# Sampled tokens: keys turned by transposes of 128 columns, weights times values on four column groups, memory values as the stationary operand

## The chip, the cores and the metric

The kernel runs on one core of a Trainium2 chip. The metric is the device time of one execution in microseconds (us). TensorE multiplies: it holds a stationary operand (at most 128 rows by 128 columns) that a weight load puts there, and streams a moving operand past it; the result lands in PSUM, on the partitions that belong to the stationary operand's columns. VectorE (DVE), ScalarE (ACT) and GpSimd (POOL) do the rest of the arithmetic, SyncE (SP) issues most DMAs, and each engine works through its own instructions in order.

## The reference

The program is one inference step of a two-layer decoder: 1024 prompt tokens, and 8 sampled tokens (one for each of 8 sequences) that stand behind a cache of 8192 tokens. Each layer projects the normalized input, runs four groups of heads side by side, and projects their gated results back. Cut to what matters for a sampled token:

```python
def nsa_mix(q, kc, vc, ks, vs, kw, vw, ...):     # 4 heads of 64, one key head
    kcc, vcc = compress_rows(kc, ...), compress_rows(vc, ...)   # 32 tokens -> 1 row
    p_c = masked_softmax(q . kcc); o_c = p_c @ vcc
    idx = top_k(score(p_c), 16)                   # 16 blocks of 64 tokens
    o_s = softmax(q . ks[idx]) @ vs[idx]          # selected tokens
    o_w = softmax(q . kw) @ vw                    # last 512 tokens
    return gates . (o_c, o_s, o_w)
# memory head, per sequence: 4 heads of 64, 256 memory rows
o_m = softmax(q . k_mem) @ v_mem
```

Every sequence has caches of its own, so for the 8 sampled tokens the keys and values differ while there are only 4 query rows (heads) for each.

## The kernel before

Each layer has a projection stage, prompt attention, a stage that compresses the paged cache (tiles `ct`, `ch`, `R`: gathered rows are transposed and multiplied with the compression weights), and an output stage in which the prompt rows go through the output weights in three products of high and low halves (tile `oa`, lines 120 to 122). The sampled tokens' work is laid between these: the window branch (`sample_window`, tile `W`) and the memory head (`mem_sample`) in the compression stage, the compressed and selected branches (`sample_select`, tiles `Vc`, `G`, `H`) in the output stage. A scheduler with priorities and a simulated timeline of its own sets each engine's order when the program is built, so an edit moves other work too.

`s_tokens` takes two samples at a time. Keys lie as tokens by 64; scores need them as 64 by tokens, the even sample's on partitions 0 to 63 and the odd one's on 64 to 127 of one PSUM tile `mt`. The even ones are transposes (`tr`, L246), the odd ones products of the key tile with an identity (L948). One fp32 product leaves two records in the trace, one transpose leaves one. All 32 query rows (8 samples by 4 heads) then meet each pair of samples with zeros where sample and query do not match.

`s_pv` transposes the weights (`PT`) and multiplies them, 32 columns wide, with the values of all 8 samples side by side, 512 columns, chunk after chunk into partitions 0 to 31 of tile `ma` (L908). A row's own sample is one of the eight blocks of 64; VectorE masks with `g4` (`oh`, L913) and adds up the blocks (`pvx`, L916). The new token's share comes from a small product (L911), which VectorE adds (L918). Per layer the function runs on 2 chunks of `Vc`, 4 chunks of `W`, and 6 of `G` with 2 of `H`.

`mem_sample` multiplies weights into the values on GpSimd (L1204), adds the two chunks of 128 rows (L1205), and sums over rows on TensorE with a column of ones as moving operand (L1207). Its result `msoy` is stored to a buffer `od` in HBM, which the output stage reads back (`oo` for prompt rows, `so` for the sampled ones, with `oz` and `sz` from the gates); `wof` are the output weights, `ox` the residual.

Of the kernel before, what the change touches and what calls it, by code (L numbers as in the profile page):

```python
# [9 lines left out]
F32 = mybir.dt.float32  # L10
# [6 lines left out]
OP = mybir.AluOpType  # L17
AX = mybir.AxisListType
# [6 lines left out]
NB = 8  # L25
# [15 lines left out]
def _const_array():  # L41
    cols = {}
    parts = []
    at = 0

    def put(name, a):
        nonlocal at
        a = np.asarray(a, np.float32)
        full = np.zeros((128, a.shape[1]), np.float32)
        full[:a.shape[0]] = a  # L50
        cols[name] = (at, a.shape[1])
        parts.append(full)
        at += a.shape[1]

    i = np.arange(128)
    put("ident", np.eye(128))
    put("causT", (i[:, None] <= i[None, :]))
    t = 128 * np.arange(NT)[None, :] + i[:, None]
    n = np.arange(32)
    put("vcmp", (t >= 31))  # L60
    inv = (10000.0 ** (-np.arange(32, dtype=np.float64) / 32)).astype(np.float32)
    pos = np.concatenate([t, np.full((128, 1), 8192)], 1).astype(np.float32)
    ang = (pos[:, :, None] * inv[None, None, :]).astype(np.float64)
    b32 = np.arange(32) // 4
    put("g4", b32[:, None] == np.arange(8)[None, :])
    put("moff", np.where(b32[:, None] == np.arange(8)[None, :], 0.0, NEG))
    put("iota64", np.tile(np.arange(64), (8, 1)))
    put("tok2", (2 * (i % 64))[:, None])
    put("i32", (i % 32)[:, None])
    put("bd16", np.repeat(np.eye(8), 16, 1))  # L70
    w = np.array([[2, 8], [4, 16]])[i // 64]
    put("invw", 1.0 / w)
    cnt = np.minimum(w[:, :, None], np.arange(16)[None, None, :] + 1)
    put("invc", (1.0 / cnt).reshape(128, -1))
    put("bones", (i[:, None] // 64) == (i[None, :] // 64))
    at1 = at
    put("mcmp", np.where(32 * n[None, None, :] + 31 <= t[:, :, None], 0.0, NEG).reshape(128, -1))
# [35 lines left out]
class Net:  # L113
# [772 lines left out]
    def s_pv(self, P, ks, V, sc, sp, new=None):  # L886


        nc = self.nc
        nch, full = len(ks), ks.count(128)  # L890
        PT = sp.tile([128, nch, 32], F32, name=f"PT{nch}")
        ps = self.psT()
        at = 0
        for c, k in enumerate(ks):
            self.tr(ps[:k, c * 32:c * 32 + 32], P[:, at:at + k])
            at += k
        if new is not None:
            self.tr(ps[:NB, nch * 32:nch * 32 + 32], P[:, at:])
            pnT = sp.tile([NB, 32], F32, name="pnT")
            nc.vector.tensor_copy(pnT, ps[:NB, nch * 32:nch * 32 + 32])  # L900
        nc.vector.tensor_copy(PT[:, :full].rearrange("p c q -> p (c q)"), ps[:, :full * 32])
        if full < nch:
            k = ks[full]
            nc.vector.tensor_copy(PT[:k, full:].rearrange("p c q -> p (c q)"), ps[:k, full * 32:nch * 32])

        O = self.psA()
        for c, k in enumerate(ks):
            nc.tensor.matmul(O[:32], PT[:k, c], V(c), start=c == 0, stop=c == nch - 1)  # L908
        pn = ps[:32, 448:512]
        if new is not None:  # L910
            nc.tensor.matmul(pn, pnT, new, start=True, stop=True)  # L911
        t = sp.tile([32, NB, 64], F32, name="oh", bufs=1)
        nc.vector.tensor_tensor(t, O[:32].rearrange("p (b d) -> p b d", d=64),  # L913
                                self.c("g4")[:32].unsqueeze(2).to_broadcast([32, NB, 64]), op=OP.mult)
        x = sp.tile([32, 64], F32, name="pvx", bufs=1)
        nc.vector.tensor_reduce(x, t.rearrange("p b d -> p d b"), axis=AX.X, op=OP.add)  # L916
        if new is not None:
            nc.vector.tensor_tensor(x, pn, x, op=OP.add)  # L918
        nc.vector.scalar_tensor_tensor(self.s_R, x, sc, self.s_R, op0=OP.mult, op1=OP.add)

    def s_tokens(self, K, V, ks, br, grp, sp):

        nc = self.nc
# [11 lines left out]
        for p in range(nb // 2):  # L935
            for S, (c0, m) in zip(Sg, cs):
                ln = sum(m)
                kh, kl = [sp.tile([128, 512], F32R, name=f"kt{x}", tag=f"kt{x}", bufs=2) for x in "hl"]
                ps = self.psT()
                for e in range(2):  # L940
                    at = 0
                    for c, k in enumerate(m):
                        to = ps[e * 64:e * 64 + 64, at:at + k]
                        x = K(2 * p + e, c0 + c)
                        if e == 0:
                            self.tr(to, x)
                        else:
                            nc.tensor.matmul(to, x, self.ident[:k, :k], start=True, stop=True)  # L948
                        at += k
                nc.scalar.copy(kh[:, :ln], ps[:, :ln])  # L950
                nc.vector.tensor_tensor(kl[:, :ln], ps[:, :ln], kh[:, :ln].bitcast(F32), op=OP.subtract)
# [13 lines left out]
    def sample_window(self, l, sp):  # L965
        W = sp.tile([128, NB, 4, 128], F32, name="W")
        for b in range(NB):
            self.nc.sync.dma_start(W[:, b], self.a["cache_nsa_win"][l, b].rearrange("(c p) k o d -> p c (k o d)", p=128))
        self.s_tokens(lambda b, c: W[:, b, c, 0:64], lambda c: W[:, :, c, 64:], [128] * 4, 2, (0, NB), sp)

    def sample_select(self, l, grp, sp):

# [43 lines left out]
        nc.vector.tensor_copy(ptf, pti)  # L1016
        for c in range(2):
            cs = slice(8 * c, 8 * c + 8)
            oh = sp.tile([32, NB, 64], F32, name="oh", bufs=1)[:nb]
# [26 lines left out]
        for b in range(nb):  # L1046
# [9 lines left out]
        self.s_tokens(lambda b, c: G[:, b, c // 2, c % 2, 128:192] if c < 6 else H[:, b, c % 2, 0:64],  # L1056
                      lambda c: G[:, :, c // 2, c % 2, 192:] if c < 6 else H[:, :, c % 2, 64:], [128] * 6 + [96] * 2, 1, grp, sp)

    def sample_out(self, sp):
# [111 lines left out]
    def mem_sample(self, l, wk):  # L1171
# [26 lines left out]
        PT = wk.tile([128, 2, 32], F32, name="msPT")  # L1198
        nc.vector.tensor_copy(PT.rearrange("p c q -> p (c q)"), pt[:, :64])

        O = self.psA()
        for b in range(NB):
            v = V[:, b].rearrange("p c (h d) -> p c h d", d=64)
            nc.gpsimd.tensor_tensor(v, v, PT[:, :, b * 4:b * 4 + 4].unsqueeze(3).to_broadcast([128, 2, 4, 64]), op=OP.mult)  # L1204
            nc.gpsimd.tensor_tensor(V[:, b, 0], V[:, b, 0], V[:, b, 1], op=OP.add)  # L1205
            for hp in range(2):
                mm(O[:, hp * NB + b:hp * NB + b + 1], V[:, b, 0, hp * 128:hp * 128 + 128], self.ones[:, 0:1],  # L1207
                   start=True, stop=True)
        oy = wk.tile([128, 2, NB], F32, name="msoy")
        nc.vector.tensor_copy(oy.rearrange("p c b -> p (c b)"), O[:, :2 * NB])  # L1210
        for c in range(2):
            self.oput(6 + c, T, NB, oy[:, c])

# [587 lines left out]
```

## Time and profile before

| what | value |
|---|---|
| median of 3 runs | 2343.73 us (2340.57 to 2345.09) |
| the profiled execution | 2343.6 us, its span 2341.8 us |
| TensorE busy | 87% of the span (weight loads 78%) |
| VectorE, ScalarE, GpSimd busy | 65%, 38%, 32% |
| mean granted TensorE clock | 0.93 |
| chain that ended last | TensorE 58%, VectorE 16%, DMA 11% |

The span runs from the first to the last instruction of the profiled execution; 1.8 us of its time lie around it. A busy share is an average over stages. The chain is followed back from the last instruction: at each step it goes to what released that instruction, or to the one before it on its engine.

### The profile page before, as it was taken

The page shows a single profiled execution, that of the slowest core. Times are in us where ns is not written, and L with a number is a line of the kernel's source. Part 1 is how long each engine was busy: PE and PEld are TensorE (multiplying, and loading weights), DVE is VectorE, ACT ScalarE, POOL GpSimd, SP SyncE. Part 2 cuts the span into 40 slices and gives each one's busy share as a digit, 9 for nine tenths or more (in the row PEclk, how much of TensorE's full clock was granted, in tenths as well). Part 3 has the DMA queues.
Part 4 walks back from the last instruction along what each step waited for, and adds up shares of the span by engine and source line. Part 5 has one row for each costly group of instructions (what it writes and reads, how often), then busy time and mean ns, then how long its engine had stood idle before and what let it go on. Part 6 is the DMA issues. An engine that isn't in the chain of part 4 may idle for free.

```text
span 2341.8 us, 41952 instructions
## 1 busy us (share of the span) xinstructions
PE 2048.5 (87%) x14396; PEld 1824.7 (78%) x14396; DVE 1511.6 (65%) x3927; ACT 888.2 (38%) x2221; POOL 746.7 (32%) x841
## 2 busy tenths in 40 slices
PE   4999998894798999896979999898949899998878
PEld 4997888784788888785669979887838888878645
DVE  7874377885777666553298724788867776656523
ACT  4223366553433323230152234675545333333101
POOL 2002123313655543223020012243146555532340
PEclk8999999997899899898989999999969998998889
DMA  7237321106655446776253363221086544467661
GB/s 249 92 109 184 94 78 52 58 26 169 176 146 149 119 125 184 201 235 200 87 171 105 112 155 98 66 61 47 28 208 170 140 135 136 138 190 221 174 206 51
DMA packets 324093, 312.97 MB, mean 134 GB/s; under 512 B 60619, under 2 KB 285783, under 8 KB 323608
## 3 DMA queue, kind: packets, MB, share of 16 engines
q1 hardware_dynamic: 261544, 213.25, 31.1%
q0 software_dynamic: 24320, 79.71, 11.7%
q10 hardware_dynamic: 38016, 17.32, 2.8%
q8 instruction: 115, 1.88, 0.3%
q14 instruction: 98, 0.80, 0.1%
HBM read 255.00 MB, written 59.57 MB: 134 GB/s over the span
## 4 chain that ended last, share of the span: by engine, by line
PE 58%; DVE 16%; DMA 11%; issue 8%; ACT 3%; POOL 2%; SPq 2%; ACTq 0%; DVEq 0%; another core or an unknown queue 0%; POOLq 0%
PE ch L120 3%; PE ch L122 3%; PE mt L246 3%; PE ct L246 3%; PE ch L121 3%; PE aa L121 3%; PE aa L122 3%; PE aa L120 3%; PE mt L1429 2%; PE oa L122 2%; PE oa L120 2%; PE oa L121 2%; DVE P L804 2%; PE fa L120 2%; PE fa L122 2%
## 5 line engine op out<-in xcount | busy, mean ns | idle before, releaser
L524 POOL DMA_INDIRECT R<-in_cache_nsa_dram,idxc x256 | 253.1, 989 | 295.8 <-PE ct L246 192.5
L120 PE MATMUL ch<-w1h,Xh 128*128 128x256 f32 x1024 | 314.3, 307 | 17.6 <-ACT Xh L564 8.7
L122 PE MATMUL ch<-w1h,Xl 128*128 128x256 f32 x1024 | 311.4, 304 | 6.1 <-DVE Xl L565 3.2
L121 PE MATMUL ch<-w1l,Xh 128*128 128x256 f32 x1024 | 308.7, 301 | 0.4 <-issue 0.4
L120 PEld LDWEIGHTS ch<-w1h,Xh 128*128 128x128 f32 x1024 | 209.1, 204 | 23.5 <-ACT Xh L564 10.2
L122 PEld LDWEIGHTS ch<-w1h,Xl 128*128 128x128 f32 x1024 | 208.4, 204 | 13.8 <-DVE Xl L565 5.7
L148 POOL TENSOR_TENSOR wl<-wf,wh 128x1024 fp32r<-128x1024 f32 (+2 forms) x42 | 94.9, 2271 | 377.1 <-ACT wh L139 295.6
L564 ACT CAST Xh<-ct 128x512 fp32r<-128x512 f32 x256 | 146.0, 585 | 180.0 <-PE ct L246 109.9
L121 PEld LDWEIGHTS ch<-w1l,Xh 128*128 128x128 f32 x1024 | 209.0, 204 | 2.0 <-issue 0.4
L565 DVE TENSOR_TENSOR Xl<-ct,Xh 128x512 fp32r<-128x512 f32 x256 | 172.4, 683 | 42.8 <-ACT Xh L564 26.1
L246 PE MATMUL ct<-cst,R 128*128 128x128 f32 x1024 | 163.9, 292 | 40.7 <-DVE Xl L565 31.0
L246 PEld LDWEIGHTS ct<-cst,R 128*128 128x128 f32 x1024 | 122.1, 149 | 53.2 <-DVE Xl L565 33.7
L544 DVE COPY R<-R 128x256 f32<-128x256 f32 x260 | 92.5, 370 | 107.5 <-DMA R<-in_cache_nsa_dram,idxc 68.9
L121 PE MATMUL aa<-wl,hTh 128*128 128x326 f32 (+1 forms) x512 | 156.6, 307 | 5.1 <-POOL wl L148 5.1
L120 PE MATMUL aa<-wh,hTh 128*128 128x326 f32 (+1 forms) x512 | 156.4, 307 | 4.0 <-ACT wh L139 4.0
L122 PE MATMUL aa<-wh,hTl 128*128 128x326 f32 (+1 forms) x512 | 156.1, 305 | 0.0
L447 ACT ACTIVATE P<-ms,nst 128x512 f32<-128x512 f32 (+3 forms) x192 | 106.6, 557 | 78.7 <-DVE nst L777 78.0
L120 PE MATMUL fa<-hTh,wh 128*128 128x344 f32 x384 | 129.4, 337 | 4.2 <-ACT fo L381 3.9
L122 PE MATMUL fa<-hTh,wl 128*128 128x344 f32 x384 | 125.1, 326 | 0.0
L121 PE MATMUL fa<-hTl,wh 128*128 128x344 f32 x384 | 125.1, 326 | 0.0
L820 DVE TENSOR_TENSOR pl<-mt,ph 128x512 fp32r<-128x512 f32 (+1 forms) x160 | 101.2, 644 | 33.9 <-ACT ph L819 29.0
L777 DVE TENSOR_REDUCE nst<-ms 128x1 f32<-128x512 f32 (+3 forms) x192 | 98.0, 517 | 32.4 <-PE ms L774 19.2
(558 smaller groups left out, 5722.9 us busy)
## 6 DMA issues: line engine op xcount, KB each, us to landing
wf<-in_w_in_dram SPq DMA_DIRECT2D x34, 512.0 KB
R<-in_cache_nsa_dram SPq DMA_DIRECT2D x256, 64.0 KB
R<-in_cache_nsa_dram ACTq DMA_DIRECT2D x256, 64.0 KB
zd<-fo SPq DMA_DIRECT2D x48, 172.0 KB
pwf<-in_cmp_w_dram SPq DMA_DIRECT2D x32, 256.0 KB
wof<-in_w_out_dram SPq DMA_DIRECT2D x16, 512.0 KB
oo<-od SPq DMA_DIRECT2D x16, 512.0 KB
oz<-zd SPq DMA_DIRECT2D x16, 512.0 KB
```

The lines of the kernel that those rows point to most:

```text
L120: mm(out, lh, rh, start=first, stop=False)
L121: mm(out, lh, rl, start=False, stop=False)
L122: mm(out, ll, rh, start=False, stop=last)
L148: e.tensor_tensor(lo, src, hi.bitcast(F32), op=OP.subtract)
L246: self.nc.tensor.transpose(out, in_, self.ident[:in_.shape[0], :in_.shape[0]])
L447: self.nc.scalar.activation(out, S, AF.Exp, bias=nm, accum_out=sm)
L524: nc.gpsimd.indirect_dma_start(R[:, j].rearrange("p c d -> p (c d)"), None, rows, bass.IndirectOffsetOnAxis(ap=self.idxc[:, l, at + j:at + ...
L544: nc.vector.tensor_copy(Rs[:, :, :, 2], R[:, :, 0:2])
L564: nc.scalar.copy(hi, pv)
L565: nc.vector.tensor_tensor(lo, pv, hi.bitcast(F32), op=OP.subtract)
L777: nc.vector.tensor_reduce(one(nm), S, axis=AX.X, op=OP.max, negate=True)
L820: nc.vector.tensor_tensor(pl[:, :n], ps[:, :n], ph[:, :n].bitcast(F32), op=OP.subtract)
```

## The change

It has three parts. In `s_tokens` the odd sample's keys are transposed too: the transpose takes 128 columns, the 64 ahead of the keys with them (values or keys of other data, so a new argument `n` of the key functions), and so fills all 128 partitions; then the even sample's transpose writes over the lower 64. In `s_pv` the chunks go to four column groups, partitions 0, 32, 64 and 96 of `ma`, each accumulating for itself; `oh` and `pvx` get up to 128 partitions, and a product with a constant `sel32` adds the groups, into the same PSUM place to which the new token's product is then added. In `mem_sample` the values are the stationary operand and two columns of weights the moving one, two chunks accumulated: 32 products per layer in place of 16, no GpSimd, and two copies in place of one.

```diff
-            nc.tensor.matmul(O[:32], PT[:k, c], V(c), start=c == 0, stop=c == nch - 1)
+            g = c % 4 * 32
+            nc.tensor.matmul(O[g:g + 32], PT[:k, c], V(c), start=c < 4, stop=c + 4 >= nch, tile_position=(0, g))
+        t = sp.tile([128, NB, 64], F32, name="oh", bufs=1)[:n]
+        nc.vector.tensor_tensor(t, O[:n].rearrange("p (b d) -> p b d", d=64),
+                                self.c("g4")[:n].unsqueeze(2).to_broadcast([n, NB, 64]), op=OP.mult)
+        x = sp.tile([128, 64], F32, name="pvx", bufs=1)[:n]
+        nc.vector.tensor_reduce(x, t.rearrange("p b d -> p d b"), axis=AX.X, op=OP.add)
         pn = ps[:32, 448:512]
+        nc.tensor.matmul(pn, self.c("sel32")[:n], x, start=True, stop=new is None)
         if new is not None:
-            nc.tensor.matmul(pn, pnT, new, start=True, stop=True)
...
-            nc.vector.tensor_tensor(x, pn, x, op=OP.add)
-        nc.vector.scalar_tensor_tensor(self.s_R, x, sc, self.s_R, op0=OP.mult, op1=OP.add)
+            nc.tensor.matmul(pn, pnT, new, start=False, stop=True)
+        nc.vector.scalar_tensor_tensor(self.s_R, pn, sc, self.s_R, op0=OP.mult, op1=OP.add)
...
-                for e in range(2):
+
+                for e in (1, 0):
                     at = 0
                     for c, k in enumerate(m):
-                        to = ps[e * 64:e * 64 + 64, at:at + k]
-                        x = K(2 * p + e, c0 + c)
-                        if e == 0:
-                            self.tr(to, x)
-                        else:
-                            nc.tensor.matmul(to, x, self.ident[:k, :k], start=True, stop=True)
+                        self.tr(ps[:64 + 64 * e, at:at + k], K(2 * p + e, c0 + c, 64 * e))
                         at += k
...
-        O = self.psA()
+        O = self.psA()[:, :4 * NB].rearrange("p (c b e) -> p c b e", c=2, e=2)
         for b in range(NB):
-            v = V[:, b].rearrange("p c (h d) -> p c h d", d=64)
-            nc.gpsimd.tensor_tensor(v, v, PT[:, :, b * 4:b * 4 + 4].unsqueeze(3).to_broadcast([128, 2, 4, 64]), op=OP.mult)
-            nc.gpsimd.tensor_tensor(V[:, b, 0], V[:, b, 0], V[:, b, 1], op=OP.add)
             for hp in range(2):
-                mm(O[:, hp * NB + b:hp * NB + b + 1], V[:, b, 0, hp * 128:hp * 128 + 128], self.ones[:, 0:1],
-                   start=True, stop=True)
+                for c in range(2):
+                    mm(O[:, hp, b], V[:, b, c, hp * 128:hp * 128 + 128], PT[:, c, b * 4 + 2 * hp:b * 4 + 2 * hp + 2],
+                       start=c == 0, stop=c == 1)
```

The order of the instructions moves with it, in three places of which the prediction speaks. Line numbers of the change stand one or two higher for what is unchanged (`tr` is L247, the output products L121 to L123). TensorE, layer 1's output stage, the first two samples' keys (`G` and `H`) between the output products. Before:

```order
L246 MATMUL mt<-cst,G 64x128 x2
L121 MATMUL oa<-wol_26769,oyh 128x512
L122 MATMUL oa<-woh_26768,oyl 128x512
L246 MATMUL mt<-cst,G 64x128 x2
L246 MATMUL mt<-cst,H 64x96
L948 MATMUL mt<-cst,G 64x128 x2
L246 MATMUL mt<-cst,H 64x96
L120 MATMUL oa<-woh_26774,oyh 128x512
```

And with the change:

```order
L918 MATMUL mt<-pvx,cst 32x64
L247 MATMUL mt<-cst,G 128x128 x4
L247 MATMUL mt<-cst,G 64x128 x4
L247 MATMUL mt<-cst,G 128x128 x2
L247 MATMUL mt<-cst,H 128x96 x2
L247 MATMUL mt<-cst,G 64x128 x2
L247 MATMUL mt<-cst,H 64x96 x2
L121 MATMUL oa<-woh_26765,oyh 128x512
```

The pair's keys now stand as one block, the odd sample's first, where they were spread over pieces with output products between them; the product L918 stands ahead of the block.

TensorE, layer 1, the last weights times values, with the tail of the program behind them (L1573, later L1572, are the sampled rows' output products). Before:

```order
L121 MATMUL oa<-wol_26775,oyh 128x512
L908 MATMUL ma<-G,PT_27626 32x512 x6
L908 MATMUL ma<-H,PT_27626 32x512 x2
L911 MATMUL mt<-vn_8_20357,pnT 32x64
L122 MATMUL oa<-woh_26774,oyl 128x512
L1573 MATMUL oa<-woh_26744,sy 40x512
```

With the change, where 22 output products stand between the first two groups of these rows:

```order
L122 MATMUL oa<-wol_26714,oyh 128x512
L911 MATMUL ma<-G,PT_27630 32x512 x6
L911 MATMUL ma<-H,PT_27630 32x512 x2
L123 MATMUL oa<-woh_26713,oyl 128x512
...
L1572 MATMUL oa<-wol_26754,sy 40x512
L918 MATMUL mt<-pvx,cst 32x64
L920 MATMUL mt<-vn_8_20359,pnT 32x64
L1572 MATMUL oa<-woh_26759,sy 40x512
```

The products on the values moved ahead of 22 output products and 4 of the sampled rows' (20 of which follow L920), which stand between them and the product L918 that needs VectorE's fold.

SP's queue at the start of layer 0's output stage. Before:

```order
L621 DMA kctd<-ko 64x128
L622 DMA vcd<-vo 128x64
L1548 DMA wof<-in_w_out_dram 128x1024
L1561 DMA oo<-od 128x8x128
L1562 DMA oz<-zd 128x8x128
L1548 DMA wof<-in_w_out_dram 128x1024 x2
L1562 DMA oz<-zd 128x8x128
L1561 DMA oo<-od 128x8x128
L1548 DMA wof<-in_w_out_dram 128x1024 x2
L675 DMA od<-msoy 128x8 x2
```

And with the change:

```order
L622 DMA kctd<-ko 64x128
L623 DMA vcd<-vo 128x64
L676 DMA od<-msoy 128x8 x2
L1563 DMA ox<-in_x_prompt_dram 128x1024 x2
L1581 DMA so<-od 128x6x8
L1582 DMA sz<-zd 128x8x8
L1547 DMA wof<-in_w_out_dram 128x1024 x3
L1560 DMA oo<-od 128x8x128
L1561 DMA oz<-zd 128x8x128
```

The store of `msoy` and the four transfers behind it moved from behind the first five weight transfers to ahead of all of them; in layer 1 they stay behind. On TensorE of layer 0 the memory products (32, L1204) stand before the last 20 transposes `ct<-R`, where the 16 products L1207 were spread between `ch` products behind those transposes.

## Rows read from the trace of the kernel before

**Rows 1.** The page: span, busy time by engine, the chain by engine

```profile
span 2341.8 us, 41952 instructions
...
PE 2048.5 (87%) x14396; PEld 1824.7 (78%) x14396; DVE 1511.6 (65%) x3927; ACT 888.2 (38%) x2221; POOL 746.7 (32%) x841
...
PE 58%; DVE 16%; DMA 11%; issue 8%; ACT 3%; POOL 2%; SPq 2%; ACTq 0%; DVEq 0%; another core or an unknown queue 0%; POOLq 0%
```

**Rows 2.** Windows: length, busy us (and instructions), granted clock, DMA share, GB/s

```profile
908.00:936.00 28.00, 26.69 (x209) 23.50 (x208) 15.29 (x40) 9.98 (x21) 7.60 (x8) 1.00 0.72 195
2240.00:2260.00 20.00, 10.48 (x51) 6.46 (x50) 1.52 (x3) 0.00 (x0) 15.26 (x16) 0.81 0.90 273
2272.00:2319.00 47.00, 47.00 (x236) 35.42 (x235) 14.77 (x24) 7.75 (x12) 0.00 (x0) 0.99 0.27 95
```

**Rows 3.** Identity products of one tile: ns min/median/max, first and last start

```profile
L948 PE MATMUL mt<-cst,G x96: 269/273/371, 1085.7 to 2299.3; 128*64 128x128 f32 x96
```

**Rows 4.** Timeline of TensorE, layer 1's output stage: start us, us, line

```profile
2292.12 0.48 PE L122 MATMUL oa<-woh,oyl 128*128 128x512 f32 x1
2292.44 0.38 PE L246 MATMUL mt<-cst,G 128*64 128x128 f32 x2
2292.66 0.33 PE L246 MATMUL mt<-cst,H 96*64 96x96 f32 x2
2292.77 0.48 PE L120 MATMUL oa<-woh,oyh 128*128 128x512 f32 x1
2293.09 0.40 PE L121 MATMUL oa<-wol,oyh 128*128 128x512 f32 x1
2293.32 0.40 PE L122 MATMUL oa<-woh,oyl 128*128 128x512 f32 x1
...
2294.01 0.40 PE L122 MATMUL oa<-woh,oyl 128*128 128x512 f32 x1
2294.34 0.65 PE L948 MATMUL mt<-cst,G 128*64 128x128 f32 x4
2294.92 0.50 PE L120 MATMUL oa<-woh,oyh 128*128 128x512 f32 x1
2295.26 0.40 PE L121 MATMUL oa<-wol,oyh 128*128 128x512 f32 x1
```

**Rows 5.** Chain of waits, products of weights and values: start us, us, what

```profile
935.73 3.55 PE ma L908 x8
...
2236.47 1.83 PE ma L908 x4
...
2319.73 6.99 PE ma L908 x16
```

**Rows 6.** Timeline of TensorE, eight records on two column groups

```profile
622.60 0.70 PE L1373 MATMUL ma<-hv,hkt 128*64 128x64 f32 x8
```

**Rows 7.** VectorE's folding of the result, grouped by line

```profile
L913 DVE TENSOR_TENSOR oh<-ma,cst x6: 678/680/681, 939.3 to 2326.8; 32x512 f32<-32x512 f32 x6
L916 DVE TENSOR_REDUCE pvx<-oh x6: 1037/1055/1062, 940.0 to 2328.0; 32x64 f32<-32x512 f32 x6
```

**Rows 8.** GpSimd's two groups in the memory head

```profile
L1204 POOL TENSOR_TENSOR msV<-msV,msPT x16: 1042/1132/2021, 994.1 to 2172.9; 128x512 f32<-128x512 f32 x16
L1205 POOL TENSOR_TENSOR msV<-msV x16: 719/734/1717, 1002.1 to 2184.8; 128x256 f32<-128x256 f32 x16
```

**Rows 9.** Timeline of TensorE, memory head of layer 1

```profile
2179.20 1.39 PE L1207 MATMUL ma<-ones,msV 128*128 128x1 f32 x12
...
2184.22 2.72 PE L1207 MATMUL ma<-ones,msV 128*128 128x1 f32 x12 [1.06 <-POOL msV L1205]
```

**Rows 10.** Chain of waits: layer 0's output stage begins; layer 1's memory head

```profile
1001.13 7.26 DMA oz<-zd
...
2178.25 5.92 POOL msV L1205 x4
...
2190.49 5.87 DMA sz<-zd
```

More of the change, by code (lines that the diff above doesn't have):

```diff
@@ L64, in _const_array @@
     b32 = np.arange(32) // 4
-    put("g4", b32[:, None] == np.arange(8)[None, :])
+    put("g4", (i % 32 // 4)[:, None] == np.arange(8)[None, :])
+    put("sel32", (i % 32)[:, None] == np.arange(32)[None, :])
     put("moff", np.where(b32[:, None] == np.arange(8)[None, :], 0.0, NEG))
@@ L906, in s_pv @@
         O = self.psA()
+        n = 32 * min(4, nch)
         for c, k in enumerate(ks):
-            nc.tensor.matmul(O[:32], PT[:k, c], V(c), start=c == 0, stop=c == nch - 1)
+            g = c % 4 * 32
[5 more added lines that the diff above has]
+        nc.vector.tensor_reduce(x, t.rearrange("p b d -> p d b"), axis=AX.X, op=OP.add)
         pn = ps[:32, 448:512]
+        nc.tensor.matmul(pn, self.c("sel32")[:n], x, start=True, stop=new is None)
         if new is not None:
-            nc.tensor.matmul(pn, pnT, new, start=True, stop=True)
[L912 to L917, printed above, removed]
-            nc.vector.tensor_tensor(x, pn, x, op=OP.add)
-        nc.vector.scalar_tensor_tensor(self.s_R, x, sc, self.s_R, op0=OP.mult, op1=OP.add)
+            nc.tensor.matmul(pn, pnT, new, start=False, stop=True)
+        nc.vector.scalar_tensor_tensor(self.s_R, pn, sc, self.s_R, op0=OP.mult, op1=OP.add)
     def s_tokens(self, K, V, ks, br, grp, sp):
@@ L968, in sample_window @@
             self.nc.sync.dma_start(W[:, b], self.a["cache_nsa_win"][l, b].rearrange("(c p) k o d -> p c (k o d)", p=128))
-        self.s_tokens(lambda b, c: W[:, b, c, 0:64], lambda c: W[:, :, c, 64:], [128] * 4, 2, (0, NB), sp)
+        self.s_tokens(lambda b, c, n: W.rearrange("p b c d -> p (b c d)")[:, (4 * b + c) * 128 - n:(4 * b + c) * 128 + 64], lambda c: W[:, :, c, 64:], [128] * 4, 2, (0, NB), sp)
     def sample_select(self, l, grp, sp):
@@ L1018, in sample_select @@
             cs = slice(8 * c, 8 * c + 8)
-            oh = sp.tile([32, NB, 64], F32, name="oh", bufs=1)[:nb]
+            oh = sp.tile([128, NB, 64], F32, name="oh", bufs=1)[:nb]
             nc.vector.tensor_tensor(oh, hf[:, 0, cs].unsqueeze(2).to_broadcast([nb, 8, 64]),
@@ L1055, in sample_select @@
         self.s_pv(Pc, [128, 128], lambda c: Vc[:, c::2], gT[:, 0:1], sp)
-        self.s_tokens(lambda b, c: G[:, b, c // 2, c % 2, 128:192] if c < 6 else H[:, b, c % 2, 0:64],
+        self.s_tokens(lambda b, c, n: G[:, b, c // 2, c % 2, 128 - n:192] if c < 6 else
+                      H.rearrange("p b y c -> p (b y c)")[:, (2 * b + c % 2) * 128 - n:(2 * b + c % 2) * 128 + 64],
                       lambda c: G[:, :, c // 2, c % 2, 192:] if c < 6 else H[:, :, c % 2, 64:], [128] * 6 + [96] * 2, 1, grp, sp)
@@ L1199, in mem_sample @@
         nc.vector.tensor_copy(PT.rearrange("p c q -> p (c q)"), pt[:, :64])
-        O = self.psA()
+        O = self.psA()[:, :4 * NB].rearrange("p (c b e) -> p c b e", c=2, e=2)
         for b in range(NB):
-            v = V[:, b].rearrange("p c (h d) -> p c h d", d=64)
-            nc.gpsimd.tensor_tensor(v, v, PT[:, :, b * 4:b * 4 + 4].unsqueeze(3).to_broadcast([128, 2, 4, 64]), op=OP.mult)
-            nc.gpsimd.tensor_tensor(V[:, b, 0], V[:, b, 0], V[:, b, 1], op=OP.add)
             for hp in range(2):
-                mm(O[:, hp * NB + b:hp * NB + b + 1], V[:, b, 0, hp * 128:hp * 128 + 128], self.ones[:, 0:1],
-                   start=True, stop=True)
+                for c in range(2):
+                    mm(O[:, hp, b], V[:, b, c, hp * 128:hp * 128 + 128], PT[:, c, b * 4 + 2 * hp:b * 4 + 2 * hp + 2],
+                       start=c == 0, stop=c == 1)
         oy = wk.tile([128, 2, NB], F32, name="msoy")
-        nc.vector.tensor_copy(oy.rearrange("p c b -> p (c b)"), O[:, :2 * NB])
+        for e in range(2):
+            hs = slice(e * 64, e * 64 + 64)
+            nc.vector.tensor_copy(oy[hs], O[hs, :, :, e])
         for c in range(2):
```

## The prediction

> **What bounds the kernel now.** I read the page first: TensorE is busy for 87% of the span of 2341.8 us and carries 58% of the chain that ended last; VectorE is at 65%, GpSimd at 32% [rows 1]. So a saving on TensorE is time only where TensorE is full, and GpSimd's work is time only where somebody waits for it. The windows say where. While the window branch's keys are turned in layer 0, TensorE is busy for 26.69 of 28 us; in the second part of layer 1's output stage for 47.00 of 47 at a granted clock of 0.99. Between them lies a hole: from 2240 to 2260 it is busy for 10.48 of 20 us, while GpSimd (15.26) issues the gathers into `G` and the DMA engines are at 0.90 [rows 2]. The gathers are not part of the change; I expect the hole to stay, and count savings at full value in the rest of the output stage and at a discount in the compression stage, where VectorE and the gathers take turns with TensorE. The timeline then gave the price of each operation, and the chain which of them it runs through: all the products of weights and values are on it [rows 5].
>
> **Keys.** Between output products the pitch from one product to the next is 0.23 us (2293.09 to 2293.32). Two transposes of `G` and two of `H` stretch the three starts 2292.12, 2292.77, 2293.09 to 0.97, so they cost 0.97 - 0.46 = 0.51, 0.13 us each, and 0.11 in the middle of a run (2292.44 to 2292.66 for two). Two identity products, four records, stretch 2294.01 to 2295.26: 1.25 - 0.46 = 0.79, or 0.40 each [rows 4]. With 0.11 a record (a record lasts 273 ns by its row, but they overlap [rows 3]) 0.44 of it is the records and 0.35 a fixed price of the run, paid going in and out. An output stage has 32 identity products in 9 runs (layer 0) and 11 (layer 1): 64 x 0.11 + 10 x 0.35 = 10.5 us. As transposes they cost 32 x 0.11 to 0.13 = 3.5 to 4.2; I take a saving of 6.8. The window branch has 16 in 4 runs: 4.9 against 1.8 to 2.1, a saving of 3.0. That a 128-column transpose costs no more than a 64-column one is from the same pitch of both kinds; at the worst it costs like a record plus half a fixed price at each change of width (a rival, below).
>
> **Weights times values.** The chain has 3.55 us for the window's 8 records, 1.83 for `Vc`'s 4, 6.99 for the 16 of `G` and `H` [rows 5]. What four column groups do is not in the trace with 512 columns. The nearest row is a product of two column groups with 64 moving columns: its eight records take 0.70 us in all [rows 6], against 0.65 for four records of a product on one group [rows 4]; the second four cost 0.05. So groups run beside each other. If four do, 6.99 becomes 1.75, 3.55 becomes 0.89, and `Vc`, which has only two chunks, goes from 1.83 to 0.92: savings of 5.2, 2.7 and 0.9. Bounds: nothing if records of 512 columns queue, and these. I take the full overlap. The Trainium skill ("TensorE: Matmul & The Clock Gate", Part 3, Measured speedup vs the span model) gives three column tiles of 512 a factor of 2.38, 0.79 of the ideal; by that the three would be 4.8, 2.4 and 0.7, and the sum 1.8 us smaller. No row here shows three or four.
>
> Against it stands the new product that adds the groups, with its own fixed price of about 0.35, twice in an output stage and once in the window branch: 0.7 and 0.35. The new token's product is there in both. It waits for the fold on VectorE, 0.68 and 1.06 us [rows 7]; In the order shown 22 output products and 4 of the sampled rows' cover the last one, at 0.23 some 6 us; behind `Vc` stand 24. Without this cover the wait of 1.74 would be paid each time. The fold itself has the same free size, and its last addition falls away, off TensorE.
>
> **Memory head.** GpSimd loses 8 x 1.13 + 8 x 0.73 = 15 us per layer, more in layer 1, where a multiplication reaches 2.02 [rows 8]. TensorE gets 32 products of two records in place of 16: twelve records take 1.39 at full clock, 0.11 each [rows 9], so 32 more cost 3.5 us. In layer 0 I count these, +3.5: nothing waited for GpSimd there. In layer 1 the chain waits 5.92 for GpSimd's additions [rows 10], and the last twelve records came after a wait of 1.06, at the lower clock (2.72 us) [rows 9]. Between 0 and -8.6 for that piece, +3.5 for the products: I take -2.5, since the next in line is the transfer `sz` of 5.87 us [rows 10], which starts after the store of `msoy`.
>
> **Sum.** Output stage: -6.8 - (5.2 + 0.9) + 0.7 = -12.2 per layer, -24.4. Window branch: -3.0 - 2.7 + 0.35 = -5.35 per layer, of which I count two thirds, -7.1 for both. Memory: +1.0. Together -30.5 on the profiled execution's 2343.6 (span and 1.8 us around it; the median is 2343.73, the same): 2313 us, -1.3%.
>
> **Rivals.**
> A, the sum, 2305 to 2321: 0.56.
>
> B, the column groups share something at 512 columns. Serial, the two terms are gone: 12.2 in the output stages and two thirds of 5.4 in the windows, 15.8 less, 2329; half the overlap gives 2321. For it: the row of two groups has only 64 columns. 0.13.
>
> C, changes of width cost. The new blocks change between 128 and 64 columns up to 24 times in an output stage and 8 in the window branch. At half of 0.35 each, 32 x 0.17 = 5.4 per layer, 2324. Against it: a run of 64-column transposes between 128-column output products paid 0.51 - 0.38 = 0.13 for going in and out [rows 4], or 0.06 a change. 0.07. The Trainium skill ("TensorEngine Tiling (Array Packing)", Key Properties) says that a change of tiling mode drains TensorE, and this is what it would do here; the runs of identity products agree, those of transposes hardly.
>
> D, the hole swallows what was saved ahead of it: the gathers' end sets when TensorE goes on, so the window branch, `Vc` and the first pair's keys count for nothing. What follows the hole, 5.2 and three quarters of 6.8, less 0.35, is 10 per layer; with the memory head's +1.0 the time is 2324. For it: 10.48 of 20 us. Against it: output products are ready to run at any time. 0.09.
>
> E, the side that ends not faster: layer 0's output stage starts later. Its chain there is already bound by transfers (7.26 us for `oz` [rows 10]), and SP now puts the store of `msoy`, and four transfers, ahead of all of `wof`. Each us by which `msoy` is late makes `wof` and all behind it one later. It cancels the sum from 26 us on and ends slower than before by 0.2% (4.7 us, about what this measurement can tell) from 35. For it: six transfers of the queue at the front, and memory products in front of 20 transposes of `R`. Against it: the memory weights were ready when GpSimd began its first multiplication at 994.1 [rows 8], and 3.5 us of products more is no 26. I give 0.15, more than this one mechanism deserves, as the scheduler moves hundreds of other rows on TensorE: 0.08 within 0.2%, 0.07 slower.
>
> **Numbers.** A to D all end faster by more than 4.7 us: 0.85. The likeliest is A, 2313. Range: with all of the window branch counted (3.6 more) and layer 1's memory head at its bound (2.6 more) the sum gives 2307; I go 7 below it, to 2300, for VectorE, which may run freer without GpSimd, and for other moves of the order. Above, 2336 holds B to D with the same 7 over the worst of them, and leaves E out.
>
> **What the profile after would show.** Keys: no identity products, 128-column transposes 0.11 apart, no gaps of 0.3 around them (C if there are). Values: the 16 records of `G` and `H` within 2 us, starting in fours a few ns apart (B if 0.43 apart). Memory: no GpSimd rows, 64 records in 7 us, no wait for them in layer 1. Chain: in layer 0 `oz` or `wof` from about 1001; if it begins past 1006, E is at work. The hole: again about 20 us; if the output products before the gathers' end only wait longer, D. The prediction is wrong if two of B, C and D hold together, or if another stage's order has got worse.

## The result, and the profile after

The changed kernel takes 2316.51 us (median of 7; 2309.97 to 2330.29), the kernel before 2340.57 in the same job (7; 2334.29 to 2353.32): a ratio of 0.9891, 95% interval 0.9858 to 0.9924, 18 to 33 us less. The forecast was 2313, a saving of 30.5 us.

The page of the changed kernel, the lines that answer to [rows 1]:

```profile
span 2314.7 us, 41899 instructions
...
PE 2018.0 (87%) x14376; PEld 1820.9 (79%) x14376; DVE 1508.7 (65%) x3925; ACT 888.5 (38%) x2221; POOL 705.6 (30%) x809
...
PE 56%; DVE 16%; DMA 10%; issue 9%; POOL 4%; ACT 3%; SPq 1%; another core or an unknown queue 1%; ACTq 0%; DVEq 0%; POOLq 0%
```

TensorE was relieved of 30.5 us of busy time, GpSimd of 41; the span is 27.1 us shorter, and TensorE's share stays at 87%. The chain of waits of the changed kernel (start us, us, what), first in layer 0, then in layer 1; it answers to [rows 5] and [rows 10]:

```profile
925.88 1.06 PE ma L911 x8
...
986.34 10.75 PE ma L1204 x64
997.10 2.66 PE ct L247 x12
...
1020.67 5.31 DMA wof<-in_w_out_dram
...
1029.47 3.74 DMA oo<-od
...
2157.01 10.66 PE ma L1204 x64
...
2216.85 0.98 PE ma L911 x4
...
2224.09 1.80 PE mt L247 x16
...
2292.54 1.86 PE ma L911 x16
...
2300.99 4.77 PE oa L1572 x20
```

The weights times values are what the sum took them for: 16 records in 1.86 us (6.99 before), `Vc`'s four in 0.98 (1.83), the window's eight in 1.06 (3.55). The block of a pair's keys, 16 transposes with three changes between 128 and 64 columns, takes 1.80, or 0.11 each. The memory products are not: 10.75 and 10.66 us for 64 records, where the sum had 7. In layer 0 the chain then goes to the output weights' transfer and to that of `oo`. The timeline shows how the last weights times values fill their 1.86 us (start us, us, line):

```profile
2292.15 0.39 PE L122 MATMUL oa<-wol,oyh 128*128 128x512 f32 x1
2292.47 1.48 PE L911 MATMUL ma<-G,PT 128*32 128x512 f32 x10
2293.36 0.60 PE L911 MATMUL ma<-H,PT 96*32 96x512 f32 x2
2293.78 0.60 PE L911 MATMUL ma<-G,PT 128*32 128x512 f32 x2
2293.80 0.60 PE L911 MATMUL ma<-H,PT 96*32 96x512 f32 x2
2294.32 0.50 PE L123 MATMUL oa<-woh,oyl 128*128 128x512 f32 x1
```

The first twelve records stand within about 1.5 us though each lasts 0.59: four on four column groups side by side, and the next four 0.43 later. The windows of the changed kernel (length, busy us of TensorE, of its weight loads, VectorE, ScalarE and GpSimd, each with its instructions, then granted clock, DMA share, GB/s):

```profile
986.00:997.00 11.00, 11.00 (x69) 11.00 (x67) 0.92 (x2) 0.87 (x3) 0.00 (x0) 0.64 0.03 7
997.00:1003.00 6.00, 6.00 (x30) 6.00 (x31) 2.58 (x6) 1.76 (x3) 0.00 (x0) 0.51 0.42 122
1003.00:1008.00 5.00, 5.00 (x45) 5.00 (x44) 2.71 (x7) 2.00 (x5) 0.00 (x0) 1.00 0.97 261
2157.00:2167.70 10.70, 10.70 (x66) 10.70 (x65) 8.19 (x10) 4.52 (x8) 0.00 (x0) 0.64 0.67 200
2167.70:2174.00 6.30, 6.30 (x22) 5.15 (x22) 1.00 (x4) 0.37 (x1) 0.00 (x0) 0.53 0.59 197
2226.00:2248.00 22.00, 5.06 (x11) 2.56 (x10) 0.15 (x1) 0.00 (x0) 13.23 (x14) 0.63 0.72 217
2249.00:2292.00 43.00, 43.00 (x216) 34.93 (x215) 17.35 (x28) 8.65 (x14) 0.00 (x0) 0.96 0.35 119
```

The first and the fourth line are the memory products, each with 128 stationary columns to load for two moving ones; the weight loads are busy as long as the products. The granted clock averages 0.64 of full speed in both, and 0.51 and 0.53 in the 6 us behind them, where transposes of `R` (12 in 2.66 us, 0.22 each) and output products (0.43 from one to the next, 0.23 in [rows 4]) mostly ran at the lower of the two levels, 1.2 in place of 2.4 GHz, before it rose again. Two of these products in layer 1:

```profile
2170.02 0.63 PE L121 MATMUL oa<-woh,oyh 128*128 128x512 f32 x1
2170.45 0.63 PE L122 MATMUL oa<-wol,oyh 128*128 128x512 f32 x1
```

The window from 2226 is the hole while `G` is gathered, 5.06 us busy of 22. The kernel before has the same hole; the window of [rows 2] begins 8 us ahead of it. Its timeline in the hole (in brackets the idle time ahead of an instruction; "issue" means that TensorE waits for nothing that the profile shows):

```profile
2258.18 0.37 PE L246 MATMUL mt<-cst,G 128*64 128x128 f32 x1 [2.54 <-issue]
2260.42 0.59 PE L121 MATMUL oa<-wol,oyh 128*128 128x512 f32 x1 [1.87 <-issue]
```

Behind the hole, in the last window, TensorE is full again. One wait, on TensorE between 985 and 1062 us of the changed kernel (us in total, times, longest), stands at 1035 us, where layer 0's output stage begins:

```profile
PE oa L121 <- DVE ox L1619: 3.1, 1, 3.1
```

### The profile page after: what moved, and what is told of

It reads as the page before. It is cut to its first block, busy times and chain, and to the rows that moved or that the text cites. A ratio compares the mean times of both kernels' runs of the same rounds, so it can differ in the third digit from the quotient of the medians.

```text
span 2314.7 us, 41899 instructions
## 1 busy us (share of the span) xinstructions
PE 2018.0 (87%) x14376; PEld 1820.9 (79%) x14376; DVE 1508.7 (65%) x3925; ACT 888.5 (38%) x2221; POOL 705.6 (30%) x809
## 4 chain that ended last, share of the span: by engine, by line
PE 56%; DVE 16%; DMA 10%; issue 9%; POOL 4%; ACT 3%; SPq 1%; another core or an unknown queue 1%; ACTq 0%; DVEq 0%; POOLq 0%
PE ch L121 3%; PE ch L123 3%; PE mt L247 3%; PE ch L122 3%; PE ct L247 3%; PE aa L123 3%; PE aa L122 3%; PE aa L121 3%; DMA R<-in_cache_nsa_dram 2%; PE oa L121 2%; PE oa L123 2%; DVE P L805 2%; PE oa L122 2%; PE mt L1428 2%; PE fa L121 2%
## 5 line engine op out<-in xcount | busy, mean ns | idle before, releaser
L121 PE MATMUL ch<-w1h,Xh 128*128 128x256 f32 x1024 | 313.7, 306 | 15.6 <-ACT Xh L565 7.8
L123 PE MATMUL ch<-w1h,Xl 128*128 128x256 f32 x1024 | 311.6, 304 | 13.8 <-issue 5.4
L123 PEld LDWEIGHTS ch<-w1h,Xl 128*128 128x128 f32 x1024 | 209.5, 205 | 21.7 <-issue 8.3
L121 PEld LDWEIGHTS ch<-w1h,Xh 128*128 128x128 f32 x1024 | 209.7, 205 | 21.0 <-ACT Xh L565 8.5
L247 PE MATMUL ct<-cst,R 128*128 128x128 f32 x1024 | 165.2, 293 | 38.7 <-DVE Xl L566 28.7
L247 PEld LDWEIGHTS ct<-cst,R 128*128 128x128 f32 x1024 | 123.3, 150 | 51.0 <-DVE Xl L566 31.5
L121 PE MATMUL aa<-wh,hTh 128*128 128x326 f32 (+1 forms) x512 | 155.9, 306 | 5.3 <-ACT wh L140 5.3
L545 DVE COPY R<-R 128x256 f32<-128x256 f32 x260 | 87.7, 351 | 104.0 <-DMA R<-in_cache_nsa_dram,idxc 63.8
L123 PE MATMUL aa<-wh,hTl 128*128 128x326 f32 (+1 forms) x512 | 155.3, 304 | 0.0
L121 PE MATMUL fa<-hTh,wh 128*128 128x344 f32 x384 | 128.5, 335 | 4.0 <-ACT fo L382 3.7
L123 PE MATMUL fa<-hTh,wl 128*128 128x344 f32 x384 | 124.2, 324 | 0.0
```

Source lines behind the costliest of these rows:

```text
L121: mm(out, lh, rh, start=first, stop=False)
L123: mm(out, ll, rh, start=False, stop=last)
L247: self.nc.tensor.transpose(out, in_, self.ident[:in_.shape[0], :in_.shape[0]])
L545: nc.vector.tensor_copy(Rs[:, :, :, 2], R[:, :, 0:2])
```

## The experiments

To see where each kernel wins or loses I matched rows of the same name in two traces, took start minus start in the kernel before, and the median of that over the rows of a stretch. The differences of these medians from stretch to stretch (us, negative is shorter) are the columns below: W is layer 0's window branch (from 880 to 965 us of the kernel before), T the rest of layer 0's compression stage (to 1047), O0 layer 0's output stage (to the projection behind it), C1 layer 1's compression stage (1780 to 2125), T1 its end (to 2200), O1 the rest. One profile each; what lies before 880 and between O0 and C1 is left out, so a row does not add up to the whole difference.

```
kernel                          W     T    O0    C1    T1    O1   ratio (95%)
whole change                 -5.5   8.1 -15.0   5.3  -4.0 -12.1   0.9891 (0.9858-0.9924)
e5 whole change again        -5.0   9.1 -13.8   1.8  -5.1 -13.5   0.9897 (0.9862-0.9933)
e1 keys                      -2.8   0.2  -9.4   2.5  -7.1  -7.9   0.9884 (0.9851-0.9917)
e2 values                    -5.3  -3.2  -3.5   6.7  -0.7  -4.6   0.9923 (0.9896-0.9950)
e3 memory                    -1.1   9.0   3.5 -20.3  -2.1   0.5   0.9973 (0.9951-0.9994)
e4 keys, values              -5.8   3.7 -10.1 -12.0  -1.8  -8.6   0.9829 (0.9800-0.9858)
e8 values, memory            -4.3   5.9  -2.9  -1.2  -8.2  -1.6   0.9987 (0.9963-1.0012)
e6 whole, other order         1.7  -1.9 -10.8  -2.8  -1.4 -10.2   0.9896 (0.9861-0.9932)
e7 memory on groups          -1.9   1.6 -15.4 -10.2  -3.7 -14.5   0.9877 (0.9830-0.9925)
```

How far one profile stands for a kernel, two of its lines say: the first two are one kernel, and differ by up to 3.5 us in a stretch. Larger differences without a cause occur: e1 gains 7.1 us in T1, where no key is turned. Between 220 and 590 us, where no part of the change lies, the nine differ from the kernel before by -3.8 to +2.6 us.

**e1, the keys alone.** The identity products of [rows 3] become transposes, the odd sample's first; nothing else changes:

```diff
...
-                        if e == 0:
-                            self.tr(to, x)
-                        else:
-                            nc.tensor.matmul(to, x, self.ident[:k, :k], start=True, stop=True)
+                        self.tr(ps[:64 + 64 * e, at:at + k], K(2 * p + e, c0 + c, 64 * e))
...
```

> The keys alone: odd samples' keys by transposes, weights times values and the memory head as before. By the sum (theory 1): 6.8 us less in each output stage and two thirds of 3.0 in each window branch, 17.6 us in all, a ratio of about 0.9925; the 32 transposes of an output stage 0.11 us apart with no fixed price at the change of width. If changes of width drain TensorE (rival), about 7 us less and a ratio of 0.997, with gaps of 0.17 us inside the blocks. Order moves may shift either by 5 us.

2318.33 against 2342.3, ratio 0.9884: 27 us where 17.6 were expected, with 9.4 and 7.9 in the two output stages where 6.8 were. No price for changes of width is seen. Of the 10 us beyond the forecast 3.7 lie in the output stages and 7.1 in T1, which the keys do not explain.

**e2, the values alone.**

```diff
-            nc.tensor.matmul(O[:32], PT[:k, c], V(c), start=c == 0, stop=c == nch - 1)
+            g = c % 4 * 32
+            nc.tensor.matmul(O[g:g + 32], PT[:k, c], V(c), start=c < 4, stop=c + 4 >= nch, tile_position=(0, g))
...
```

> Weights times values on four column groups alone. By the sum: 6.1 less 0.7 in each output stage, two thirds of 2.35 in each window branch, 14 us in all, ratio 0.994; the 16 records of G and H within 1.9 us. If the column groups were only half as good as they look in the changed kernel's profile because the keys' blocks stand elsewhere there, 7 us and 0.997.

2327.5, ratio 0.9923, about 18 us; 3.5 and 4.6 in the output stages (5.4 expected), 5.3 in the window branch.

**e3, the memory head alone.**

```diff
-            nc.gpsimd.tensor_tensor(v, v, PT[:, :, b * 4:b * 4 + 4].unsqueeze(3).to_broadcast([128, 2, 4, 64]), op=OP.mult)
-            nc.gpsimd.tensor_tensor(V[:, b, 0], V[:, b, 0], V[:, b, 1], op=OP.add)
...
+                    mm(O[:, hp, b], V[:, b, c, hp * 128:hp * 128 + 128], PT[:, c, b * 4 + 2 * hp:b * 4 + 2 * hp + 2],
+                       start=c == 0, stop=c == 1)
...
```

> The memory head alone: values as stationary, no GpSimd. Theory 1: the run of 64 records costs 10.7 us in each layer, as in the changed kernel, since the granted clock falls in it, and what follows runs at the lower clock for some us more; GpSimd's 15 us were hidden in layer 0. Layer 0 loses 8 us at the end of the compression stage, layer 1 between 0 and 3: ratio 1.002 to 1.005. Rival: GpSimd freed pays for it, layer 1 gains 6 and layer 0 loses 3.5, ratio 0.999. The gain of 3 to 4 us that the changed kernel shows before 220 us, where nothing was changed, should not come back if it is chance.

2334.98, ratio 0.9973, outside what theory 1 (1.002 to 1.005) and its rival (0.999) gave. Layer 0 loses 9.0 us in T, as theory 1 said, but the kernel as a whole is not slower: in C1, ahead of layer 1's memory products, its profile is 20 us shorter, where only the order of the work was changed. (This profile is the fastest of the twelve executions.) In the first 220 us it differs by 0.1 us from the kernel before: what the whole change's first profile gained there was chance.

**e4, keys and values without the memory part** (the diffs of e1 and e2 together).

> The change without its memory part. Theory 1: the sum of the first two kernels, 30 us less than before, a ratio of 0.986 to 0.988, some 5 to 8 us faster than the whole change. Rival: the memory part helps, and this is 2 to 5 us slower than the whole change, ratio 0.991. The 7 us that the whole change lost in layer 1's compression stage between 1900 and 2045 us: if they come from the memory part they are gone here; if from the order alone, they may stand in any of the four.

2305.51, ratio 0.9829, 37 us less than before and 15 less than the whole change by the two ratios. That is more than theory 1 had (0.986 to 0.988). T loses 3.7, not 8 to 9, and C1 gains 12.

**e5, the whole change again**, without an edit.

> The whole change once more, as the control for the next two and for how far one profile stands for a kernel. If the 7 us that it lost between 1900 and 2045 us of the first profile belong to its order, they stand there again; if they are chance of one execution, they do not. Ratio 0.986 to 0.992.

2314.7, ratio 0.9897. The loss between 1900 and 2045 us that I had seen in the first profile was chance for the most part: C1 is 1.8 in this one.

**e6, the same work in another order.** The memory head is written ahead of the window branch:

```diff
-                        self.sample_window(l, pool(s2, "sw"))
-                    with ExitStack() as s2:
                         self.mem_sample(l, pool(s2, "ms", 2))
+                    with ExitStack() as s2:
+                        self.sample_window(l, pool(s2, "sw"))
```

> The whole change with the same work, but the memory head handed to the scheduler ahead of the window branch, so that the order of layer 1's compression stage comes out another way. Theory 1 (order): the loss of 7 us in layer 1's compression stage goes or turns into a gain, 5 to 15 us faster than the whole change, ratio 0.983 to 0.987; the memory products still take 10.7 us in each layer. Rival (the memory part's work itself costs the 14 us by which the whole change is slower than keys and values alone): no change from the whole change, 0.989.

2315.21, ratio 0.9896, the whole change's: theory 1 (0.983 to 0.987) missed, its rival was met. The memory products moved some 30 us up in layer 0, into W, which lost its gain, and T is free of them (together -0.2, where the whole change has 2.6 and 4.1). C1 came out at -2.8, near the whole change's two; in layer 1 the memory products now begin at 2103.6 us of this profile, where C1 ends.

**e7, another memory head.** The weights of all queries are stationary, 32 columns, on the column group of the sample; 256 columns of values move; `gm` masks head and sample, and products with `sel32` add the groups:

```diff
-        O = self.psA()[:, :4 * NB].rearrange("p (c b e) -> p c b e", c=2, e=2)
...
+        for q in range(0, 512, 256):
+            for c, b in ((c, b) for c in range(2) for b in range(q // 64, q // 64 + 4)):
+                g = b % 4 * 32
+                mm(O[g:g + 32, q:q + 256], PT[:, c], V[:, b, c], start=c == 0, stop=c == 1, tile_position=(0, g))
...
+        nc.vector.tensor_tensor(t, O.rearrange("p (b d) -> p b d", d=64),
+                                self.c("gm")[:].unsqueeze(2).to_broadcast([128, NB, 64]), op=OP.mult)
...
+        nc.vector.tensor_reduce(x, t.rearrange("p b d -> p d b"), axis=AX.X, op=OP.add)
...
+        for e in range(2):
+            mm(R[e * 64:e * 64 + 64, :32], x, self.c("sel32"), start=True, stop=True, tile_position=(0, e * 64))
...
```

> The whole change with another memory head: the weights, 32 columns, stationary on four column groups and the values of four samples moving, 256 columns each; VectorE masks and folds, two products with the selection constant add the groups. 16 products per layer in fours, about 2 us in place of the run of 10.7, and no fall of the granted clock with it. Theory 1: 8 us less in each layer on TensorE, of which layer 0 gives back some to its output weights' transfers: 8 to 16 us faster than the whole change in the same order of layer 1 (that of the other-order kernel), ratio 0.978 to 0.982. Rival: the run of the memory products was hidden beside transfers, no gain over the other-order kernel.

2310.23, ratio 0.9877. Theory 1 wanted 0.978 to 0.982 and missed; the interval (0.9830 to 0.9925) holds the whole change's ratio too, so the times do not tell the two memory heads apart. The timeline of this kernel in layer 0:

```profile
1001.51 0.62 PE L248 MATMUL ct<-cst,R 128*128 128x128 f32 x4
1002.07 1.93 PE L1205 MATMUL ma<-msV,msPT 128*32 128x256 f32 x32
1003.93 1.09 PE L248 MATMUL ct<-cst,R 128*128 128x128 f32 x8
```

32 records in 1.93 us in place of 64 in 10.75, and its windows there, in the columns of before, keep the full clock:

```profile
999.00:1004.00 5.00, 5.00 (x59) 3.76 (x58) 2.47 (x6) 1.81 (x5) 0.00 (x0) 1.00 0.06 13
1004.00:1010.00 6.00, 6.00 (x53) 5.83 (x54) 4.05 (x8) 2.34 (x5) 0.00 (x0) 1.00 0.03 3
```

T costs 1.6. In layer 1 the two products with `sel32` stand right behind the others in TensorE's queue, and TensorE waits for VectorE's fold, uncovered, which the column of waits (last) shows:

```profile
2159.88 1.93 PE L1205 MATMUL ma<-msV,msPT 128*32 128x256 f32 x32
2165.04 0.43 PE L1213 MATMUL mt<-cst,msx 128*64 128x32 f32 x4 [3.23 <-DVE msx L1210]
```

**e8, values and memory.**

> Values and memory without the keys; its order in layer 1's compression stage is that of the whole change and of the values alone. Theory 1: the values' gain (0.9923) less 6 to 8 us for the memory run: 0.995 to 0.996, with the same loss of some 7 us between 1900 and 2045 as both of these. Rival (memory alone is 6 us faster than before, and stays so beside the values): 0.990.

2337.36, ratio 0.9987 (0.9963 to 1.0012); both forecasts (0.995 to 0.996, and 0.990) missed. T loses 5.9. Alone the two parts gave 0.9923 and 0.9973; together they give nothing that can be measured. The memory part is thus worth 6 us alone and -15 beside the values: its own price in T is there both times (9.0, and 5.9 against e2's -3.2). Where the rest of the -15 stands the profiles cannot show: the span of this one is only 2.7 us longer than e2's. In this kernel the store of `msoy` stays behind the first three transfers of `wof`, as before (SP's queue, us):

```profile
994.85 2.61 SPq L1550 DMA_DIRECT2D wof<-in_w_out_dram  x2
1005.45 0.81 SPq L676 DMA_DIRECT2D od<-msoy  x2
```

The last job ran on a chip on which the kernel before takes 2271.13 us, 69 less. Its ratios are told by themselves. The kernel before was not profiled there, so the columns of these four profiles still compare with the profile of the first job, where it takes 69 us more.

**e9, keys and values again.**

> Keys and values without the memory part, once more, on the chip of the next three. If layer 1's compression stage (1780 to 2125 us of the kernel before) again comes out some 12 us shorter than in the kernel before, where the whole change's two profiles lost 5 and 2, its order is the reason, and the ratio is again 0.983; if not, that was chance, and the ratio is 0.986 to 0.988.

2253.69, ratio 0.9933 (0.9907 to 0.9958): only 17 us, outside both forecasts. C1 is -14.4, T 3.6, much as in e4. Where the missing 20 us lie these profiles cannot show.

**e10, the memory head on column groups again**, e7's kernel.

> The whole change with the memory head on column groups, once more, since its interval was wide (0.983 to 0.9925). If the memory run's 10.7 us in layer 0 is what the whole change pays, this stands within 0.002 of keys and values alone; if something else of the memory part costs, it stays at 0.988.

2264.22, ratio 0.9958 (0.9931 to 0.9986), 0.0025 above e9, whose interval overlaps; neither forecast is met. T is 2.9; C1 is 1.9, 16 us behind e9's. The same kernel had -10.2 there as e7, so one kernel's C1 differs by 12 us from profile to profile.

**e11, e10's work with the memory head ahead of the window branch**, the edit of e6.

> The same kernel as the one before, with the memory head handed to the scheduler ahead of the window branch: same work, another order. If the work decides, within 0.003 of the one before; if the order does, further off. The best guess for the fastest of all: 0.981 to 0.985.

2240.51, ratio 0.9870 (0.9834 to 0.9906), short of the best guess but the fastest of this chip and 24 us faster than e10 with the same work: here the order decides as much as the whole change did, where the same edit gave nothing in e6. T is 3.5, without the memory products, which moved into W as in e6; C1 is -8.1, T1 -17.9 (e10: -4.5).

**e12, the memory part alone, one more profile.**

> The memory part alone, one more profile. Its first one showed layer 1's compression stage 20 us shorter than the kernel before, and was the fastest of its 12 executions, 10 below their median. If that stage's order is the reason, it is again 15 to 20 shorter; if chance, it is within 8 of the kernel before.

One time of 2288.35, 17 us above the median of the kernel before on this chip and above all 23 of its times (to 2282.78), where e3 was 6 us faster than the kernel before. T is 9.2, C1 -8.6: part of the 20 us of its first profile was chance, part may be order. Its output stages, which it does not change, show what is different on this chip. The windows of e3 and of e12 over the stretch in which GpSimd issues the gathers, each first in layer 0 and then in layer 1:

```profile
1098.00:1118.00 20.00, 5.39 (x18) 2.86 (x17) 1.16 (x3) 0.59 (x1) 12.49 (x13) 0.60 0.73 219
2229.00:2250.00 21.00, 4.80 (x16) 2.46 (x14) 0.84 (x2) 0.00 (x0) 12.55 (x14) 0.64 0.72 222
```

```profile
1088.00:1109.00 21.00, 20.72 (x115) 14.45 (x114) 6.94 (x10) 3.88 (x6) 16.12 (x17) 1.00 0.92 276
2207.00:2228.00 21.00, 20.48 (x109) 14.25 (x108) 6.35 (x10) 3.40 (x6) 16.12 (x17) 1.00 0.93 283
```

On the first chips TensorE is busy for 4.80 to 5.39 of some 20 us, here for 20.48 to 20.72 of 21. The hole of [rows 2] is gone. Without it, other waits appear. TensorE's waits in the same stretch of layer 0 (us in total, times, longest), first of e9, then of e12, which has the old order of the keys:

```profile
PE ms L951 <- DVE ktl L949: 4.2, 2, 3.8
PE mt L247 <- DMA G<-in_cache_nsa_dram,idx: 1.4, 1, 1.4
```

```profile
PE mt L948 <- DMA G<-in_cache_nsa_dram,idx: 0.8, 2, 0.5
```

With the keys of a pair in one block TensorE waits for the gathers of the pair's second sample, and 3.8 us at one go for the low halves of a later pair's keys on VectorE, 5.6 us against 0.8.

## Why the prediction was right, and which terms were off

The time was right, 2313 for 2316.5, and the terms for the keys and the weights times values were close. Part of the nearness is luck: the forecast took off 30.5 us, the measured gain is 24, and the kernel before came out 3 us lower (2340.57) in this job than the 2343.6 from which the sum started. The memory head's term was too small in layer 0, and layer 1's compression stage moved by amounts that the sum did not have.

- **Values.** The step held: four column groups run side by side at 512 columns. 6.99, 3.55 and 1.83 became 1.86, 1.06 and 0.98, where 1.75, 0.89 and 0.92 were forecast. The reading behind it was thin: the row of [rows 6] has 64 moving columns, the one from [rows 4] set against it 128, and neither has four groups; that 512 columns would do the same was a bet. The 16 records give a factor of 3.8 for four groups, ahead of the 2.38 for three that the Trainium skill ("TensorE: Matmul & The Clock Gate", Part 3, Measured speedup vs the span model) gives, 0.94 of the ideal where that is 0.79. Rival B is out.
- **Keys.** 0.11 us a transpose, as forecast, and in the blocks no price for a change of width: the chain's 16 in 1.80 us hold three changes. (Rival C counted 24 changes in an output stage; in the order shown a pair has four, which makes 16.) Rival C is out. The Trainium skill's rule that a change of tiling mode drains TensorE ("TensorEngine Tiling (Array Packing)", Key Properties), with which the prediction backed C, does not say whether these transposes change the mode; the trace shows no drain between them. The output stages gained 9.4 and 7.9 in e1 for 6.8 forecast.
- **Output stages together.** -12.2 each was forecast; -15.0 and -12.1, -13.8 and -13.5 were measured in the two profiles of the whole change. The hole stayed some 20 us long, but it did not hold back what was saved ahead of it, as rival D had it with 10 per layer: all four values are above 10, and in layer 1 the gathers themselves came earlier (the last one starts at 2242.3 in place of 2263.5). D is less likely, not excluded: its time of 2324, 20 us less, lies within the interval.
- **Window branch.** -5.35 per layer, counted at two thirds; W shows -5.5 and -5.0, so layer 0 realized all (-2.8 and -5.3 for the two parts alone, -5.8 for both in e4). In layer 1 it is not separable from C1.
- **Memory head, the term that was mis-sized.** "In layer 0 I count these, +3.5" failed: T costs 8.1 and 9.1 in the whole change, 9.0, 5.9 and 9.2 in e3, e8 and e12, on average 8.3, against 1.1 on average without the memory part (0.2, -3.2, 3.7, 3.6 in e1, e2, e4, e9). So the memory part costs some 7 us there, twice the term. The price of 0.11 us a record was read at full clock; in a run of 64 records the clock fell, the run took 10.75 in place of 7, and the transposes behind it ran at the lower level too. e7 and e10, whose run takes 1.9 us and keeps its clock, have 1.6 and 2.9 in T (e11's 3.5 has no memory products in it).
- **Rival E**, the store of `msoy` and the transfers behind it ahead of the output weights, can be set apart by the same runs. With the store ahead T is 8.1 to 9.2 with the long run (the whole change, e5, e3, e12) and 1.6 and 2.9 with the short one (e7, e10); with the store behind it is 5.9 with the long run (e8) and 1.1 on average without it. The run thus makes 5 to 7 us of the loss, the order of the queue 1 to 3, at one profile each. The wait of 3.1 us for `ox` fits this: e7 and e10 have one of 2.3 and 2.4. The sign set for E, a chain of transfers that begins past 1006, came (1020.67), but the first output product starts at 1019.65, ahead of 1022.41 before.
- **Memory head, layer 1.** No wait for the memory head is left, as forecast, but the gain of 2.5 cannot be told from chance: T1 is -4.0 and -5.1, and -2.1 and -8.2 in e3 and e8, against -0.7, -1.8 and -7.1 without the memory part in e2, e4 and e1.
- **What the sum did not have.** C1, where the values' and the window's edits touch only a little, moved by -20 to +7 us from kernel to kernel. Part is chance, or the chip: e3 and e12 are one kernel, -20.3 and -8.6, and so are e7 and e10, -10.2 and 1.9. That part is order is likely, not shown: e4 and e9, one kernel on two chips, have -12.0 and -14.4, against 5.3, 1.8, 6.7 and -1.2 in four profiles of three kernels (the whole change, e2, e8) that have one order over most of it. Of the 15 us by the times between e4 and the whole change, the profiles show some 5 from the memory run in T (8.1 and 9.1 against 3.7) and 14 to 17 in C1, of which the output stages and T1 take 11 to 12 back. That an order by itself can be worth as much is shown by the times of e10 and e11. What in the order makes the difference was not settled.

The hole: its cause was not found. That it is there on the chips of the first jobs and not on that of the last, in the same kernel, is shown; so is that the keys' new order pays waits of some 5 us where it is missing. That these waits are a reason why keys and values gain 17 us there and 37 elsewhere is argued, and they are too small for all of it: the output stages of e9 gained 8.6 and 5.6 more than e12's own shift (-25.9 and -26.0 against -17.3 and -20.4), where e4 had 10.1 and 8.6; by this comparison they hold 4.5 of the missing 20 us, and the rest stays open.

## What to carry to other kernels

Narrow products with stationary operands of 32 columns are best sent round the four column groups, with one small product to add the groups: at 512 moving columns this gave 3.8 of 4. A run of many products with two moving columns cost more here than its records at full clock, since the granted clock fell in it and stayed low for what followed; the same sums with the values moving on column groups took a fifth of it and kept the clock, though the whole kernel's time did not show that gain clearly. Where a scheduler orders the program, a change's gain is known no better than the order's effect, which was 24 us in one pair of runs here and nothing in another: run the same work in a second order before a part is called good or bad, as one part was worth 6 us alone and minus 15 beside another.

## What the runs showed of the hardware that was not expected

- In the run of 64 memory records, during which TensorE was never idle, the granted clock averaged 0.64, and 0.51 to 0.53 in the 6 us behind it; at 0.22 a transpose and 0.43 an output product these 6 us were mostly at the lower level, 1.2 GHz. 32 records of 256 moving columns on four groups kept 1.00 in layer 0 of e7.
- Four column groups with 512 columns of fp32 each: 16 records in 1.86 us against 6.99.
- On the chips of the first jobs TensorE issues one instruction in 2 to 3 us while GpSimd's gathers run, waiting for nothing that the profile shows (4.80 of 21 us busy), and on that of the last it does not (20.48 of 21), though GpSimd issues the 24 gathers within 29 to 31 us on both. The kernel before takes 2340 us on the one and 2271 on the other.
